# Attention in a four-branch decoder layer: values follow two score blocks behind, a third score bank, and the division and gate beside the third output pass

## The chip, the cores and the metric

One core of a Trainium2 chip runs the whole program. The metric is the device time of one execution in microseconds (us), as the median of several runs. Views of the profile come from one execution that was recorded.

## The reference, cut to what matters

One layer of a decoder takes 1024 prompt tokens and 8 sample tokens (width 2048) through one input projection, then through four groups of heads: A (gated delta rule), B (RWKV-7), C (forgetting attention) and D (pooling). Each group's output is multiplied by a gate, and one output projection with LayerNorm ends the layer. Group C and the end are what the change touches:

```python
s = jnp.einsum('nqhd,nshd->nhqs', qb, k) * (HEAD_DIM ** -0.5)
s = s + jnp.swapaxes(cqb, 1, 2)[..., :, None] - jnp.swapaxes(ck, 1, 2)[..., None, :]
s = jnp.where((kpos[None, :] <= qpos[:, None])[None, None], s, NEG_INF)
return jnp.einsum('nhqs,nshd->nqhd', jax.nn.softmax(s, axis=-1), v)
...
gated = jnp.concatenate([o_A * _silu(z_A), o_B * _silu(z_B), o_C * _silu(z_C), o_D * _silu(z_D)], axis=-1)
out = jnp.einsum('nte,ed->ntd', gated, P['w_out'])
y = _layernorm(ALPHA_DN * x + out, P['ln_g'], P['ln_b'])
```

Group C has 8 heads of 64 numbers; c is the running sum of the log forget gates. The 8 sample tokens attend to 4096 cached positions each.

## The kernel before, in words

All is float32; a product of two float32 matrices is made as three matmuls of parts (high and low: whi, wlo, xh, xl; ph, pl for the weights of the softmax). Nobody writes the order of an engine's instructions by hand: a scheduler fixes it when the program is built, from dependences, priorities and its own estimate of times. Side work ("fillers", generators given to `add` with a rate) is put between the instructions of the main work by `fill`, a few steps each time. Each engine then carries out its list in order and waits at an instruction whose inputs are late.

Stage by stage: input projection with the branches A, B and D as side work (to about 1717 us), then the attention stage `mixing` (1717 to 1920 us), then four output passes in the order D, B, A, C: three `out_pass` and `out_last`, which also does the LayerNorm.

In the attention stage `branch_c` goes through the 8 heads. In `c_attend` a head has two blocks of 512 queries; for each block of 128 keys TensorE makes the scores transposed (L849 with the low parts, L850 with the high parts and four rows of offsets, L853 or L855 the causal mask) into a PSUM bank "s", ScalarE takes the exponential into cpt (L859, three buffers) and rounds it to cph (L860), VectorE makes the remainder cpl (L861), and three matmuls L868 to L870 add weights times values into a bank "v". These value matmuls are held back by `late_values`: they come after the scores of the next LEAD blocks.

While head h runs, `c_scores(h + 2)` is a filler that prepares head h+2: loads on ScalarE's queue, ckk by GpSimd (L825, L826), and `c_max`, which finds each query's largest score. That is 12 blocks of matmuls (L785, mask L788) into banks "b" and "m", each read by a reduction on VectorE into cmx (L789); then cm (L792), a transpose on TensorE (L794), cmt on ScalarE (L796), its parts cmh and cml on VectorE (L798, L799), DMAs on ScalarE's queue (L831) into cmr, and a cast on VectorE into the offset rows of cqx (L832), in two halves of 512 queries. The scores L850 of head h+2 read cqx. A second filler, `decode_v`, streams cached values (dkv) through TensorE for the sample tokens (L1105).

The banks of `mixing` are "s", "v" and "m" with CBANKS of each, "b" with two and "k" with one. `c_max` and the value transposes ask `ctag` for a bank, which cycles over "b", "b" and "m".

When two heads are done, `c_gate` divides and gates their outputs at once: cden = exp(-log den) on ScalarE (L908), cnum times cden (L911) and times the gate cz (L912) on GpSimd over 128x1024, and a DMA into the DRAM array G (L913). An output pass reads its group's part of G with `gated` (L1694 to L1696: a load, gh on ScalarE, gl on VectorE). In the third pass VectorE adds ALPHA times x (L1714) and the sums from PSUM (L1720) to y; the weights' parts are cast by ScalarE and VectorE (L302, L303).

Of the kernel before, what the change touches and what calls it, by code (L numbers as in the profile page):

```python
# [6 lines left out]
F32 = mybir.dt.float32  # L7
# [3 lines left out]
AF = mybir.ActivationFunctionType  # L11
# [4 lines left out]
T = 1024  # L16
# [8 lines left out]
NPOOL = {392: 8, 384: 10, 256: 8}  # L25
VBUFS = 5, 4
RATE_L = 1.6
LEAD = 1
CBANKS = 2, 2, 1
RATE_C = 1.1  # L30
AHEAD = 2000
RATE_V = 0.7, 1.5
# [147 lines left out]
class Kernel:  # L180
# [14 lines left out]

    def ps(self, tag="a", shape=(128, 512)):
        pool, bufs = {"pj": (self.psum1, 3), "a": (self.psum1, 2), "o": (self.psum1, 5), "s": (self.psum1, CBANKS[0]),
                      "v": (self.psum1, CBANKS[1]), "m": (self.psum1, CBANKS[2]), "b": (self.psum0, 2), "k": (self.psum0, 1)}[tag]
        return self.t(pool, list(shape), tag, F32, bufs=bufs)

    def c(self, name, rows=slice(0, 128)):
# [702 lines left out]
        self.late_values()  # L904

    def c_gate(self, pool, hp, num, den):
        nc = self.nc
        nc.scalar.activation(den, den, AF.Exp, scale=-1.0)  # L908
        z = self.t(pool, [128, T], "cz", bufs=1)
        nc.gpsimd.dma_start(z, self.O["pj"][CZ + hp, :, :T])  # L910
        nc.gpsimd.tensor_tensor(num, num, den, op=ALU.mult)  # L911
        nc.gpsimd.tensor_tensor(num, num, z, op=ALU.mult)  # L912
        nc.gpsimd.dma_start(self.G[8 + hp, :, :T], num)  # L913


    def pages(self, pool, bufs, lead):
# [867 lines left out]
    def build(self):  # L1784
# [8 lines left out]
        self.gr = tc.dram_tile([8, N], F32, name="grow")  # L1793
        self.br = tc.dram_tile([8, N], F32, name="brow")
        self.UT = tc.dram_tile([4, 16, 32, 32], F32, name="ut")
        self.lfd = tc.dram_tile([8, 32, 1024], F32, name="lfd")
        self.crow = tc.dram_tile([8, 4, T], F32, name="crow")
        self.sco = tc.dram_tile([128, 4097], F32, name="sco")
# [7 lines left out]
        with P(name="const", bufs=1) as cp, P(name="psum", bufs=2, space=PSUM) as self.psum0:  # L1806
            with P(name="psum1", bufs=2, space=PSUM) as self.psum1:
                with P(name="w", bufs=2) as wp, P(name="x", bufs=1) as xp:
                    a, b = w(self.seq[0]), w(self.seq[1])
                    self.weights(wp, [c for p in zip(a, b) for c in p] + [c for t in self.seq[2:] for c in w(t)], 2)  # L1810
                    self.weight(0)
                    with P(name="stage", bufs=4) as sp:
                        self.load_x(xp, sp)
                        self.setup(cp, sp)
                        self.inputs(cp, sp)
                    with P(name="stage2", bufs=2) as sp:
                        self.inputs_cd(sp)
            dv = P(name="dv", bufs=1)
            vp = dv.__enter__()
            with P(name="psumc", bufs=2, space=PSUM) as self.psum1, P(name="c2", bufs=1) as c2, P(name="c1", bufs=1) as c1, \  # L1820
                    P(name="c", bufs=2) as cpool:
                self.cp += [c1, c2]
                self.mixing(vp, cpool)
            self.c0.__exit__(None, None, None)
            with P(name="psum2", bufs=2, space=PSUM) as self.psum1:
                R = dict(side="right")
                with P(name="wo", bufs=2, **R) as wp, P(name="ost", bufs=2, **R) as sp, P(name="y", bufs=1, **R) as yp, \
                        P(name="g2", bufs=1, **R) as g2:
                    self.y = [self.t(yp, [128, N], f"y{c}") for c in range(16)]
                    order = (3, 1, 0, 2)  # L1830
                    self.weights(wp, [self.I["wo"][ct][:, 4 * br:4 * br + 4] for br in order for ct in range(16)], 1, 48)
                    with P(name="g1", bufs=1) as g1:
                        g = [self.gated(3, g1, sp)]
                        with P(name="posta", bufs=1) as pp:
                            post = self.post_chain_a(pp)
                            self.add(post, RATE_P)
                            self.out_pass(0, g[0], sp)
                            self.drain(post)
                        g.append(self.gated(1, g2, sp))
                        with P(name="smpA", bufs=1) as pp:  # L1840
                            smp = self.sample_a(pp)
                            self.add(smp, RATE_P)
                            self.out_pass(1, g[1], sp)
                            self.drain(smp)
                        g.append(self.gated(0, g1, sp))
                        self.out_pass(2, g[2], sp)
                        self.drain()
                        g.append(self.gated(2, g2, sp))
                    dv.__exit__(None, None, None)
                    with P(name="wres", bufs=1) as rp:  # L1850
                        self.keep = rp
                        self.out_last(3, g[3], sp, rp)
# [63 lines left out]

    def mixing(self, vp, cpool):

        tags = itertools.cycle(("b",) * 2 + ("m",) * CBANKS[2])
        self.ctag = lambda: next(tags)  # L1920
        self.add(self.decode_v(vp), RATE_V[0])
        self.branch_c(cpool)
        for f in self.fillers:
# [43 lines left out]
```

## Time and profile before

| what | value |
|---|---|
| median of 3 runs | 2395.63 us (2390.84 to 2396.36) |
| profiled execution | 2396.94 us, of which its span on the core is 2395.2 us |
| TensorE busy over the span | 95% |
| VectorE, ScalarE, GpSimd busy | 57%, 39%, 12% |
| mean granted TensorE clock | 0.979 |

The span is the stretch from the first to the last recorded instruction; 1.74 us of the execution lie around it. A busy share averages over stages. The granted clock is 1.0 at 2.4 GHz and 0.5 at 1.2 GHz; a mean between them says how much of a stretch was spent at the lower one. An entry like "[2.31 <-DVE cmx L789]" in a row says that the engine stood idle for 2.31 us before this instruction, until VectorE's instruction of line 789 had made cmx.

### The profile page before, as it was taken

The numbers are of one execution on the slowest core, as the hardware profiler recorded it, in microseconds if no ns is written. First come the engines' busy times: TensorE is split into PE (matmuls) and PEld (weight loads), VectorE is DVE, ScalarE is ACT, GpSimd is POOL, SyncE is SP. The second block draws the span as 40 slices with busy tenths as digits, with TensorE's granted clock in tenths as the row PEclk, the third lists the DMA queues.
The fourth block names the chain that finished last, engine by engine and source line by source line (L and its number), as shares of the span: only waits on it lengthen the run. The fifth ranks groups of instructions, "written<-read, shape, count | busy, mean of one in ns | idle before, by whom it ended". The sixth has DMA issues, their size and how long they took to land. (4 is left out here: it accounts for less than half of the span.)

```text
span 2395.2 us, 47251 instructions
## 1 busy us (share of the span) xinstructions
PE 2282.6 (95%) x17640; PEld 2023.0 (84%) x17640; DVE 1364.7 (57%) x2676; ACT 938.4 (39%) x1853; POOL 295.0 (12%) x408
## 2 busy tenths in 40 slices
PE   8999999999899999999999999999899999999984
PEld 8999999998899999787787877899755578889984
DVE  4665757677576557432222245555578644564598
ACT  5644445434454444121111122454366665211244
POOL 0000000000000000103111121100132110100175
PEclk9999999999999999999999999999999999999997
DMA  6133323545523336778878888653488775683212
GB/s 215 56 100 95 104 85 95 151 106 120 113 81 94 89 107 142 172 187 264 274 250 283 259 273 288 232 161 107 124 260 248 223 282 192 219 304 129 88 63 88
DMA packets 369664, 402.44 MB, mean 168 GB/s; under 512 B 204877, under 2 KB 228350, under 8 KB 368666
## 3 DMA queue, kind: packets, MB, share of 16 engines
q1 hardware_dynamic: 307698, 263.83, 37.3%
q10 hardware_dynamic: 50056, 101.60, 13.9%
q0 software_dynamic: 11680, 33.99, 4.3%
q8 instruction: 139, 2.28, 0.4%
q14 instruction: 91, 0.75, 0.1%
HBM read 314.56 MB, written 84.67 MB: 167 GB/s over the span
## 5 line engine op out<-in xcount | busy, mean ns | idle before, releaser
L308 PE MATMUL pj<-xh,wlo 128*128 128x344 f32 x2688 | 873.1, 326 | 16.7 <-DVE wlo L303 8.6
L309 PE MATMUL pj<-xl,whi 128*128 128x344 f32 x2688 | 871.5, 324 | 0.0
L310 PE MATMUL pj<-xh,whi 128*128 128x344 f32 x2688 | 865.2, 324 | 0.0
L308 PEld LDWEIGHTS pj<-xh,wlo 128*128 128x128 f32 x2688 | 508.1, 189 | 37.1 <-issue 11.4
L309 PEld LDWEIGHTS pj<-xl,whi 128*128 128x128 f32 x2688 | 508.5, 189 | 19.8 <-issue 14.4
L310 PEld LDWEIGHTS pj<-xh,whi 128*128 128x128 f32 x2688 | 507.9, 189 | 16.4 <-issue 13.1
L302 ACT CAST whi<-raw 128x256 fp32r<-128x256 f32 (+1 forms) x504 | 213.0, 424 | 732.6 <-PE pj L310 530.2
L303 DVE TENSOR_TENSOR wlo<-raw,whi 128x256 fp32r<-128x256 f32 (+1 forms) x504 | 226.8, 452 | 365.5 <-ACT whi L302 356.1
L309 PE MATMUL o<-gl,whi 128*128 128x344 f32 x576 | 185.8, 323 | 0.0
L308 PE MATMUL o<-gh,wlo 128*128 128x344 f32 x576 | 184.6, 325 | 0.8 <-ACT gh L1695 0.5
L310 PE MATMUL o<-gh,whi 128*128 128x344 f32 x576 | 185.1, 321 | 0.0
L308 PEld LDWEIGHTS o<-gh,wlo 128*128 128x128 f32 x576 | 107.9, 188 | 21.8 <-DVE y L1720 9.4
L309 PEld LDWEIGHTS o<-gl,whi 128*128 128x128 f32 x576 | 109.0, 189 | 2.3 <-DVE ps L1221 0.9
L310 PEld LDWEIGHTS o<-gh,whi 128*128 128x128 f32 x576 | 109.0, 189 | 0.8 <-issue 0.8
L365 ACT ACTIVATE stg<-pj 128x344 f32<-128x344 f32 x168 | 74.6, 457 | 74.2 <-PE pj L310 73.0
L997 PE MATMUL k<-dkv,dqb 128*32 128x256 f32 x1024 | 88.4, 394 | 15.1 <-DMA dkv<-in_ck 9.0
L1720 DVE TENSOR_TENSOR y<-y,o 128x344 f32<-128x344 f32 x96 | 48.0, 510 | 57.3 <-PE o L310 57.0
L1105 PE MATMUL k<-dkv,dpT 128*8 128x512 f32 x512 | 71.5, 635 | 0.8 <-DMA dkv<-in_cv 0.8
L861 DVE TENSOR_TENSOR cpl<-cpt,cph 128x512 fp32r<-128x512 f32 (+1 forms) x96 | 60.9, 653 | 15.7 <-ACT cph L860 14.9
L308 PE MATMUL o<-gh,wkl 128*128 128x392 f32 (+2 forms) x192 | 63.9, 333 | 0.6 <-DVE wkl L303 0.5
L310 PE MATMUL o<-gh,wkh 128*128 128x392 f32 (+2 forms) x192 | 63.6, 331 | 0.0
L309 PE MATMUL o<-gl,wkh 128*128 128x392 f32 (+2 forms) x192 | 63.3, 330 | 0.0
(597 smaller groups left out, 3321.9 us busy)
## 6 DMA issues: line engine op xcount, KB each, us to landing
dkv<-in_ck SPq DMA_DIRECT2D x256, 256.0 KB
dkv<-in_cv SPq DMA_DIRECT2D x256, 256.0 KB
raw<-in_w ACTq DMA_DIRECT2D x228, 256.0 KB
out_pj<-stg ACTq DMA_DIRECT2D x33, 516.0 KB
bop<-bop SPq DMA_DIRECT2D x16, 1024.0 KB
raw<-in_wo ACTq DMA_DIRECT2D x64, 256.0 KB
aop<-aop SPq DMA_DIRECT2D x16, 768.0 KB
aop<-aost SPq DMA_DIRECT2D x40, 256.0 KB
```

The costliest lines, as they stand in the source:

```text
L302: nc.scalar.copy(hi, raw)
L303: nc.vector.tensor_tensor(lo, raw, hi.bitcast(F32), op=ALU.subtract)
L308: nc.tensor.matmul(ps, lhsT=wlo, rhs=xh, start=start, stop=False)
L309: nc.tensor.matmul(ps, lhsT=whi, rhs=xl, start=False, stop=False)
L310: self.last = nc.tensor.matmul(ps, lhsT=whi, rhs=xh, start=False, stop=stop).ins
L365: self.nc.scalar.activation(dst[:, g * G3:g * G3 + G3], ps[g], func)
L861: nc.vector.tensor_tensor(pl[:, off:], pt[:, off:], ph[:, off:].bitcast(F32), op=ALU.subtract)
L997: nc.tensor.matmul(ps[32 * hp:32 * hp + 32], lhsT=qb[:, hp, b], rhs=kt[:, :, hp], start=b == 0, stop=b == 7)
L1105: mm = lambda i: nc.tensor.matmul(po[32 * i:32 * i + 8], lhsT=pTv[:, c, :, 4 * bg + i], rhs=t[i // 2][:, i % 2], start=False, stop=c == 31)
L1720: nc.vector.tensor_tensor(y[:, s], y[:, s], ps[g], op=ALU.add)
```

## The change

`LEAD` goes from 1 to 2: the value matmuls of a block come after the scores of the next two. The score banks "s" go from two to three, and bank "m" is given up for it, so that `c_max`, its transpose and the value transposes use the two banks "b" alone. `c_gate` now only writes numerator and log denominator into two new DRAM arrays. The division and the gate become `gate_c`, a filler beside the third output pass, in eight pieces of 128x512: three loads on GpSimd's queue, an exponential, two products on GpSimd, a store into G.

```diff
-LEAD = 1
-CBANKS = 2, 2, 1
+LEAD = 2
+CBANKS = 3, 2
...
-                      "v": (self.psum1, CBANKS[1]), "m": (self.psum1, CBANKS[2]), "b": (self.psum0, 2), "k": (self.psum0, 1)}[tag]
+                      "v": (self.psum1, CBANKS[1]), "b": (self.psum0, 2), "k": (self.psum0, 1)}[tag]
...
     def c_gate(self, pool, hp, num, den):
-        nc = self.nc
-        nc.scalar.activation(den, den, AF.Exp, scale=-1.0)
-        z = self.t(pool, [128, T], "cz", bufs=1)
-        nc.gpsimd.dma_start(z, self.O["pj"][CZ + hp, :, :T])
-        nc.gpsimd.tensor_tensor(num, num, den, op=ALU.mult)
-        nc.gpsimd.tensor_tensor(num, num, z, op=ALU.mult)
-        nc.gpsimd.dma_start(self.G[8 + hp, :, :T], num)
+        self.nc.gpsimd.dma_start(self.CN[hp], num)
+        self.nc.gpsimd.dma_start(self.CD[hp], den)
+
+    def gate_c(self, pool):
+
+        nc = self.nc
+        for hp in range(4):
+            for s in (slice(0, 512), slice(512, 1024)):
+                o, d, z = (self.t(pool, [128, 512], x, bufs=2) for x in ("gn", "gd", "gz"))
+                nc.gpsimd.dma_start(o, self.CN[hp, :, s])
+                nc.gpsimd.dma_start(d, self.CD[hp, :, s])
+                nc.gpsimd.dma_start(z, self.O["pj"][CZ + hp, :, s])
+                nc.scalar.activation(d, d, AF.Exp, scale=-1.0)
+                nc.gpsimd.tensor_tensor(o, o, d, op=ALU.mult)
+                nc.gpsimd.tensor_tensor(o, o, z, op=ALU.mult)
+                nc.gpsimd.dma_start(self.G[8 + hp, :, s], o)
+                yield 1
...
-                        self.out_pass(2, g[2], sp)
-                        self.drain()
+                        with P(name="gatec", bufs=1) as pp:
+                            self.add(self.gate_c(pp), RATE_P)
+                            self.out_pass(2, g[2], sp)
+                            self.drain()
...
-        tags = itertools.cycle(("b",) * 2 + ("m",) * CBANKS[2])
-        self.ctag = lambda: next(tags)
+        self.ctag = lambda: "b"
```

The scheduler makes a new order from this. Three places of it follow. A row gives a line, an operation, what it writes and what it reads, with buffer numbers. Lines of the changed kernel are one lower than before up to the function `c_gate`, so that L784, L787, L793, L848, L849 and L867 to L869 are the L785, L788, L794, L849, L850 and L868 to L870 of before.

The first place is TensorE early in the stage, in head 0. Before, the values (v) of a block follow one block (s) behind:

```order
L849 MATMUL s_21505<-cqq_20424,ckk_20423 128x512
L850 MATMUL s_21505<-cqx_20425,ckx_20414 128x512
...
L870 MATMUL v_21349<-cpl_21345,cvh_20294 128x384
L868 MATMUL v_21349<-cph_21410,cvl_20295 128x256
L869 MATMUL v_21349<-cph_21410,cvh_20294 128x256
L870 MATMUL v_21349<-cpl_21411,cvh_20294 128x256
L868 MATMUL v_21349<-cph_21427,cvl_20295 128x256
L869 MATMUL v_21349<-cph_21427,cvh_20294 128x256
L849 MATMUL s_21522<-cqq_20424,ckk_20423 128x512
L850 MATMUL s_21522<-cqx_20425,ckx_20414 128x512
```

In the changed kernel the same stretch reads:

```order
L848 MATMUL s_21502<-cqq_20426,ckk_20425 128x512
L849 MATMUL s_21502<-cqx_20427,ckx_20416 128x512
L869 MATMUL v_21413<-cpl_21182,cvh_20296 128x512
...
L869 MATMUL v_21413<-cpl_21409,cvh_20296 128x256
L848 MATMUL s_21520<-cqq_20426,ckk_20425 128x512
L849 MATMUL s_21520<-cqx_20427,ckx_20416 128x512
L848 MATMUL s_21537<-cqq_20426,ckk_20425 128x512
L849 MATMUL s_21537<-cqx_20427,ckx_20416 128x512
L848 MATMUL s_21602<-cqq_20426,ckk_20425 128x512
L849 MATMUL s_21602<-cqx_20427,ckx_20416 128x512
```

Score blocks now stand in bunches of up to three, with the values of earlier blocks between the bunches.

The second place is TensorE at the transpose L794 of head 6, whose cqx is number 23160 (scores and values that follow are those of head 5). Before, the order goes on with score and value blocks:

```order
L794 MATMUL b_23513<-cst_211,cm_3271_23511 8x128
L785 MATMUL b_23652<-ckx_23557,cqm_23558 128x256
L788 LDWEIGHTS identb_19787
L788 MATMUL b_23652<-mq_19789,identb_19787 128x128
L870 MATMUL v_23583<-cpl_23579,cvh_22229 128x384
L868 MATMUL v_23583<-cph_23644,cvl_22230 128x256
L869 MATMUL v_23583<-cph_23644,cvh_22229 128x256
L785 MATMUL m_23733<-ckx_23557,cqm_23558 128x512
...
L849 MATMUL s_23969<-cqq_23159,ckk_23158 128x512
L850 MATMUL s_23969<-cqx_23160,ckx_23149 128x512
```

From the first of these rows to the last, which reads cqx of head 6 for the first time, there are 74. In the changed kernel (cqx number 23150) there are 17:

```order
L793 MATMUL b_23504<-cst_213,cm_3269_23502 8x128
L784 MATMUL b_23625<-ckx_23546,cqm_23547 128x256
L787 LDWEIGHTS identb_19789
L787 MATMUL b_23625<-mq_19791,identb_19789 128x128
L784 MATMUL b_23643<-ckx_23546,cqm_23547 128x256
...
L784 MATMUL b_23660<-ckx_23546,cqm_23547 128x384
...
L784 MATMUL b_23722<-ckx_23546,cqm_23547 128x512
...
L784 MATMUL b_23740<-ckx_23546,cqm_23547 128x512
L784 MATMUL b_23743<-ckx_23546,cqm_23547 128x256
...
L849 MATMUL s_23958<-cqx_23150,ckx_23139 128x512
```

The `c_max` blocks of head 7 (ckx number 23546) have moved into one bunch between the transpose and the scores of head 6.

The third place is GpSimd. Before, the two products of a head pair stand between the preparations of two heads:

```order
L777 MEMSET cmx_22709 128x16
L911 TENSOR_TENSOR cnum_21172<-cnum_21172,cden_21173 128x1024
L912 TENSOR_TENSOR cnum_21172<-cnum_21172,cz_22178 128x1024
L913 DMA gated<-cnum_21172 128x1024
L910 DMA cz_23102<-out_pj 128x1024
L825 TENSOR_TENSOR ckk_22688<-ckr_22677,ckx_22679 64x1024
```

In the changed kernel only the two writes stand there, and the products have gone behind the last DMA of the second pass (out_oAS):

```order
L906 DMA cn<-cnum_21174 128x1024
L907 DMA cd<-cden_21175 128x1024
L776 MEMSET cmx_22703 128x16
L824 TENSOR_TENSOR ckk_22681<-ckr_22670,ckx_22672 64x1024
...
L1492 DMA out_oAS<-sS_26418 128x2048
L915 DMA gn_27927<-cn 128x512
L916 DMA gd_27928<-cd 128x512
L917 DMA gz_27929<-out_pj 128x512
...
L919 TENSOR_TENSOR gn_27927<-gn_27927,gd_27928 128x512
L920 TENSOR_TENSOR gn_27927<-gn_27927,gz_27929 128x512
L921 DMA gated<-gn_27927 128x512
```

## Rows read from the trace of the kernel before

**Rows 1.** The page: span, and each engine's busy time, share and count.

```profile
span 2395.2 us, 47251 instructions
PE 2282.6 (95%) x17640; PEld 2023.0 (84%) x17640; DVE 1364.7 (57%) x2676; ACT 938.4 (39%) x1853; POOL 295.0 (12%) x408
```

**Rows 2.** Windows: attention stage, two pieces of it, passes two and three.

```profile
core 0: us, PE busy (x) PEld busy (x) DVE busy (x) ACT busy (x) POOL busy (x), PEclk, DMA share, GB/s
1717.00:1920.00 203.00, 181.58 (x1000) 106.14 (x998) 155.18 (x267) 132.00 (x258) 48.69 (x34) 0.92 0.83 249
1783.00:1807.00 24.00, 20.83 (x125) 12.75 (x126) 22.67 (x37) 16.35 (x35) 9.96 (x7) 1.00 0.89 272
1874.00:1898.00 24.00, 19.55 (x103) 11.71 (x103) 12.72 (x18) 13.64 (x29) 5.88 (x4) 0.86 0.71 217
2040.00:2246.00 206.00, 204.81 (x1345) 183.18 (x1343) 113.95 (x211) 36.01 (x61) 9.70 (x17) 1.00 0.58 195
```

**Rows 3.** Waits of PE's weight loads in 1717 to 1920: total us, times, longest.

```profile
PEld v L870 <- DVE cpl L861: 10.0, 8, 4.7
PEld s L849 <- ACT cpt L859: 8.9, 6, 2.9
PEld v L868 <- ACT cpt L859: 5.1, 6, 0.9
PEld v L868 <- ACT cph L860: 3.2, 5, 1.0
```

**Rows 4.** Timeline at a `c_gate`, all engines: start, duration, instruction, [idle before].

```profile
1834.37 2.35 POOL L911 TENSOR_TENSOR cnum<-cnum,cden 128x1024 f32<-128x1024 f32 x1 [3.27 <-ACT cden L908]
1834.96 1.91 DVE L799 TENSOR_TENSOR cml<-cmt,cmh 8x128 fp32r<-8x128 f32 x1
1836.80 0.41 DVE L789 TENSOR_REDUCE cmx<-m 128x1 f32<-128x256 f32 x1
...
1837.46 0.44 PE L785 MATMUL b<-ckx,cqm 66*128 66x384 f32 x1 [2.31 <-DVE cmx L789]
```

**Rows 5.** Timeline at the next `c_gate`, and two rows away from one.

```profile
1880.75 2.40 POOL L912 TENSOR_TENSOR cnum<-cnum,cz 128x1024 f32<-128x1024 f32 x1
1880.98 2.45 DVE L861 TENSOR_TENSOR cpl<-cpt,cph 128x256 fp32r<-128x256 f32 x1
...
1883.48 0.58 PE L870 MATMUL v<-cpl,cvh 128*128 128x256 f32 x1 [4.45 <-DVE cpl L861]
...
1731.32 0.41 DVE L861 TENSOR_TENSOR cpl<-cpt,cph 128x256 fp32r<-128x256 f32 x1
...
1860.27 0.27 DVE L799 TENSOR_TENSOR cml<-cmt,cmh 8x128 fp32r<-8x128 f32 x1
```

**Rows 6.** Windows of 10 us around those two places (columns as in rows 2).

```profile
1830.00:1840.00 10.00, 7.64 (x45) 3.92 (x43) 8.36 (x17) 7.67 (x17) 5.36 (x4) 0.89 0.80 239
1880.00:1890.00 10.00, 6.52 (x22) 3.33 (x22) 6.72 (x8) 3.94 (x7) 4.20 (x4) 0.66 0.68 216
```

**Rows 7.** Timeline: transposes and offset casts of head 6, then of head 2.

```profile
1857.59 0.27 PE L794 MATMUL b<-cst,cm 128*8 128x128 f32 x1
...
1863.09 0.42 DVE L832 CAST cqx<-cmr 4x512 fp32r<-4x512 f32 x1
...
1866.99 0.42 DVE L832 CAST cqx<-cmr 4x512 fp32r<-4x512 f32 x1
...
1762.40 0.27 PE L794 MATMUL m<-cst,cm 128*8 128x128 f32 x1
...
1770.25 0.42 DVE L832 CAST cqx<-cmr 4x512 fp32r<-4x512 f32 x1
...
1776.47 0.42 DVE L832 CAST cqx<-cmr 4x512 fp32r<-4x512 f32 x1
```

**Rows 8.** Timeline of GpSimd in 2125 to 2210, passes two and three.

```profile
2206.10 0.75 POOL L1121 DMA_DIRECT2D gated<-dzs  x1 [74.30 <-DVE dzs L1120]
```

**Rows 9.** Third pass: VectorE's y by lines, and the tile gl.

```profile
L1714 DVE SCALAR_TENSOR_TENSOR y<-ostg,y 128x1032 f32<-128x1032 f32 x16 | 19.7, 1231 | 16.6 <-DMA ostg<-in_xT 16.5
...
L309 PE MATMUL o<-gl,wkh x5: 338/342/342, 2246.7 to 2249.5; 128*128 128x392 f32 x5
L1696 DVE TENSOR_TENSOR gl<-ostg,gh x4: 1233/1234/1236, 2213.2 to 2221.6; 128x1032 fp32r<-128x1032 f32 x4
```

More of the change, by code (lines that the diff above doesn't have):

```diff
@@ L1 @@
-import itertools
 import math
@@ L1795, in build @@
         self.UT = tc.dram_tile([4, 16, 32, 32], F32, name="ut")
+        self.CN = tc.dram_tile([4, 128, T], F32, name="cn")
+        self.CD = tc.dram_tile([4, 128, T], F32, name="cd")
         self.lfd = tc.dram_tile([8, 32, 1024], F32, name="lfd")
```

## The prediction

> **What bounds the kernel now.** I read the page first: TensorE (PE) is busy for 95% of the span, VectorE (DVE) 57%, ScalarE (ACT) 39%, GpSimd (POOL) 12% [rows 1]. So a gain must come from a stretch in which PE stands still or is slowed. The windows show which. In the second and third pass PE is busy 204.81 of 206 us at granted clock 1.00 [rows 2]: there is nothing to gain there, only something to spoil. In the attention stage it is busy 181.58 of 203 us at clock 0.92 [rows 2]: about 21 us idle, and if the clock's mean of 0.92 lies between its two levels of 2.4 and 1.2 GHz, another 0.08 x 203 = 16 us of it were given up to the lower one. The change edits this stage, and moves its last step into the third pass.
>
> Inside the stage no single engine bounds. In 1783 to 1807 DVE is busy 22.67 of 24 us (94%), but in 1874 to 1898 only 12.72 (53%) with PE at 19.55 [rows 2]. So I read next the waits, which say what PE stands still for. Four of them are of the pipeline score, exponential, remainder, values: values for cpl 10.0 us, scores for the exponential that frees their bank 8.9, values for cpt and cph 5.1 and 3.2 [rows 3], together 27.2 us. Last I read the timeline where the longest ones stand.
>
> **What the change does, part by part.** (a) *GpSimd's two products leave the stage.* They are four pairs of 2.35 and 2.40 us [rows 4, 5]. At 1834.37 the first product runs, and VectorE's cml takes 1.91 us where it takes 0.27 elsewhere [rows 4, 5]; the reduction from PSUM at 1836.80 beside the next product takes 0.41, so it is not disturbed. At 1880.98 cpl takes 2.45 us where 0.41 is usual [rows 5]. What follows on PE: `c_max` stands 2.31 us for a bank whose reduction was queued behind that cml [rows 4], and the values stand 4.45 us for that cpl [rows 5]. After each, the granted clock of the 10 us is 0.89 and 0.66 [rows 6], which costs about 10 x 0.11 = 1.1 and 10 x 0.34 = 3.4 us. Sum 2.31 + 4.45 + 1.1 + 3.4 = 11.3 us. The stage also loses four exponentials of 128x1024 on ACT, which is busy 132 of 203 us [rows 2] and so gives back a little; I take −12 in all. Bounds: if other waits step in, only the excess durations come back, 1.6 + 2.0 = 3.6 us (−4); −13 if ACT's share is double.
>
> The Trainium skill (page "SBUF — State Buffer", sections "Who interferes with whom" and "SBUF: two separate sides") says that a VectorE instruction with two SBUF inputs, or a cast in a two-port mode, contends with a GpSimd instruction that reads SBUF, that the later one waits for the earlier one's whole length, and that a reduction never does on this chip. By that rule, the trace agrees: 1.91 and 2.45 us beside 0.41 for the reduction [rows 4, 5]. The rule speaks against the new place as well; it is the third rival.
>
> (b) *Values two blocks behind, and a third score bank.* Before, PE could run one block ahead of ACT and DVE; now it can run two. Of the 27.2 us of pipeline waits [rows 3], 4.45 are in (a) already, and the longest for cpt, 2.9, is the start-up of the stage, where nothing is ahead yet; 27.2 − 4.45 − 2.9 = 20 us remain. A deeper queue can remove a wait that comes from jitter, but not one where DVE is simply full, as in 1783 to 1807. I take three quarters, −15; bounds −5 (only the waits away from the full stretches) and −20.
>
> (c) *The scheduler's order gives up cover at the start of a head.* From the transpose L794 to the second cast into cqx a chain runs over ACT, DVE, a DMA, DVE, and again a DMA: head 6 needs 5.9 us to its first cast's end and 9.8 to its second; head 2 8.3 and 14.5 [rows 7] (1863.09 + 0.42 − 1857.59; the others likewise). I take head 6's, rounded to 6 and 10, since head 2's stands at the start of the stage's crowded middle. Before, 74 rows of PE's order stood between the transpose and the first score that reads cqx; now 17 stand there for head 6. What PE has to do in them: a matmul of 344 columns takes 204.81 / 1345 = 0.152 us in the passes [rows 2], so 512 columns about 0.23. The rows shown for head 6 are blocks of 256, 256, 384, 512, 512 and 256 columns and five masks of 128, 2816 columns or 1.3 us. The same count over the order of the changed kernel gives, for heads 2 to 7, 9.5, 8.0, 3.0, 5.7, 1.3 and 0.9 us up to the first score, and 15.9, 12.8, 6.3, 8.8, 5.6 and 4.1 up to the fifth block, which needs the second half. Against 6 us, heads 4 to 7 wait 3.0, 0.3, 4.7 and 5.1 = 13.1 us; against 10 us the second halves add about 0.7 for head 4, 0.9 for head 5 and little for heads 6 and 7, whose wait has already shifted them. Sum +15. With a chain shorter by a seventh it is +12; with head 2's lengths it is +35, the second rival. Three of these stalls are as long as the 4.45 us after which the clock fell; at 1.1 to 3.4 us for each [rows 6] that is 3 to 10 us, and I take +3, since the work behind them is dense.
>
> (d) *Two banks instead of three for `c_max`.* A block then needs the reduction of the block two before, 0.4 to 0.7 us of DVE. The order is alternated with other PE work nearly everywhere; where it is not, it is the bunch inside head 6's and head 7's chain, during which PE would wait for cqx anyway. Its cover is that wait, so 0; without it some 5 us.
>
> (e) *Division and gate in the third pass.* GpSimd there stands still for 74.30 us before its one DMA at 2206.10 [rows 8], so eight pieces with half the product's 2.4 us twice each, 8 x 2 x 1.2 = 19 us, have room. VectorE has 114 of 206 us of work there [rows 2]. PE needs group C's gl from 2246.7; it was ready by 2221.6 + 1.2 = 2222.8 [rows 9], so 24 us of slack hide the gate as long as the last piece is not later than that. The risk is that VectorE's two-input instruction y = ALPHA x + y (L1714), 16 x 1.231 us [rows 9], is held up by GpSimd's products; PE does not wait for y unless its five banks are all full. Bounds 0 and +6, taken +1. In the stage itself one load and one store of a head pair give way to two stores of the same size, so nothing there.
>
> **The sum.** −12 − 15 + 15 + 3 + 0 + 1 = −8 us. The profiled execution took 2396.94 us, its span of 2395.2 and 1.74 around it; it lies 1.3 us above the median of the runs, 2395.63. The same −8 from that median gives 2388 us. What a measurement of this kernel tells from no change is about 0.3%, 7.2 us; so this is just beyond it.
>
> **The rivals.** First, *the freed middle*. Where DVE is 94% busy [rows 2], c_max blocks move later, into the stretch where it is half idle, and cml, cqx and cpl lose what GpSimd added; then (b) reaches its bound of −20 and (c) its lower 12 with a clock that stays up: −12 − 20 + 12 = −20, 2375 us. For it: the uneven load of DVE. Against it: c_max of heads 6 and 7 is moved exactly into the chains.
>
> Second, and on the other side, *the chain of the offsets becomes the stage's bound*. Place: PE at the first score of heads 4 to 7. If a chain takes as long as head 2's, 8.3 and 14.5 us [rows 7], PE waits 35 us and loses 6 by the clock, against −12 and −15 and part of (b) that has nothing to hide: 35 + 6 − 12 − 14 = +15, 2411 us. It decides from a chain of about 8 us to the first cast. For it: the chain's last links are DMAs on ACT's queue and DVE casts that queue behind others' work, and head 2's was that long. Against it: every chain but that was near 6, and the products that lengthen casts are gone.
>
> Third, *the gate spoils the third pass*. GpSimd's 19 us hold VectorE's y-additions and weight casts; if each piece costs PE a stall of 1 to 1.75 us, 8 to 14 us in all, the sum becomes 0 to +6: 2396 to 2402 us. By the rule of the Trainium skill named under (a), up to 19 us of VectorE's time would be blocked there. Against it: 24 us of slack, and 16 VectorE instructions of 1.231 us in some 100 us are the only large ones with two SBUF inputs.
>
> Fourth, *nothing is gained*: the pipeline waits only move from cpl and cpt to cqx, since ACT and DVE have the same work as before. (b) at −5 and (a) at −8 against +15 and +1 give about +3; with (b) between, −4 to +3: 2392 to 2399 us.
>
> **How the numbers follow.** Forecast 0.44 (its own range 2378 to 2396), freed middle 0.14, chain as the bound 0.15, spoiled third pass 0.05, nothing gained 0.22. Faster by more than 0.3% is below 2388.4: 0.34 of the forecast's 0.44 and the 0.14, 0.48. The rest of the forecast, 0.10, and the 0.22 are within it: 0.32. Slower is above 2402.8: 0.15 and 0.05, 0.20. The range goes from 2372, a little beyond the freed middle, to 2403; the chain as the bound is left out, and some 0.02 at either end.
>
> **What would show it.** Right: beside the stage no cml, cqx or cpl above 1 us; the waits of values for cpl and of scores for cpt at a quarter of [rows 3]; PE's longest waits at the first scores of heads 4, 6 and 7, for VectorE's cqx, of 3 to 5 us each; attention stage 9 us shorter, third pass unchanged within 2 us, and gl of group C ready before its first matmul. Wrong: waits for cqx of 7 us or more, or none; waits of L784 for cmx away from these places; holes on PE in the third pass.

## The result

The changed kernel takes 2409.0 us (median of 12 runs, 2400.77 to 2416.5) where the kernel before takes 2395.99 (12 runs, 2385.15 to 2407.89): a ratio of 1.0056, 95% interval 1.0034 to 1.0077. It is slower, by 13 us. The forecast was 2388, within 2372 to 2403.

The page of the changed kernel, its span and the engines' busy time (to [rows 1]):

```profile
span 2404.5 us, 47346 instructions
PE 2291.2 (95%) x17640; PEld 2025.9 (84%) x17640; DVE 1362.4 (57%) x2676; ACT 939.6 (39%) x1857; POOL 314.3 (13%) x448
```

TensorE has as many matmuls and was busy 8.6 us longer. To see where, I cut the trace at three events: the last matmul of the projection, the last values matmul of attention, and the first matmuls of the first and of the fourth output pass. Before, that gives these windows (columns as in rows 2), the attention stretch and passes one to three:

```profile
1717.20:1919.50 202.30, 180.99 (x997) 105.81 (x996) 155.10 (x266) 131.31 (x257) 48.69 (x34) 0.92 0.83 249
1920.40:2246.50 326.10, 320.83 (x2063) 284.88 (x2064) 170.17 (x287) 104.90 (x190) 26.60 (x41) 0.99 0.61 208
```

In the changed kernel the same, with the 4 us between them, and two pieces of the attention stretch:

```profile
1716.40:1925.90 209.50, 187.00 (x979) 111.00 (x977) 148.93 (x265) 127.15 (x253) 33.47 (x28) 0.89 0.77 232
1925.90:1929.90 4.00, 3.19 (x22) 0.65 (x22) 1.58 (x4) 1.47 (x3) 1.08 (x2) 1.00 1.02 407
1929.90:2256.70 326.80, 320.11 (x2063) 283.21 (x2064) 174.30 (x286) 108.73 (x197) 60.33 (x86) 1.00 0.69 235
...
1826.00:1836.00 10.00, 8.36 (x27) 4.32 (x26) 5.30 (x11) 3.37 (x8) 0.00 (x0) 0.50 0.31 108
1876.00:1886.00 10.00, 9.78 (x36) 3.94 (x35) 6.21 (x13) 3.54 (x8) 0.00 (x0) 0.50 0.43 138
```

The passes did not move: 326.1 us and 326.8. The attention stretch and the few us behind it went from 203.2 to 213.5 us, and that is all of the loss in this execution. Idle time (length less PE's busy time) is 21.3 us before and 22.5 after. What grew is the time given up to the lower clock, length times (1 − granted clock): 202.3 x 0.08 = 16 us before, 209.5 x 0.11 = 23 us after. The two parts overlap where PE stands idle at the lower clock, so their sum is an upper bound. The two pieces show how it looks: PE is busy nearly throughout and runs at 1.2 GHz. In 1876 to 1886 it carries out 36 matmuls at that clock.

The waits of PE's weight loads in 1717 to 1930 of the changed kernel (to [rows 3]):

```profile
PEld v L869 <- DVE cpl L860: 8.5, 10, 2.1
PEld s L849 <- DVE cqx L831: 7.5, 4, 3.4
PEld b L784 <- DVE cmx L788: 5.8, 10, 1.5
PEld b L784 <- DVE cpl L860: 5.1, 5, 1.7
PEld v L867 <- ACT cph L859: 4.9, 5, 1.7
PEld s L848 <- ACT cpt L858: 3.9, 2, 2.2
...
PEld b L784 <- DVE cqx L831: 1.7, 1, 1.7
...
PEld v L867 <- ACT cpt L858: 0.9, 1, 0.9
```

Two kinds of wait have grown: scores for cqx, and `c_max` (L784) for a bank behind cmx and cpl. Scores waiting for cqx are new. Its longest case is head 7 in the timeline of the changed kernel: the transpose L793, the two casts of the offsets, and the first scores that read them:

```profile
1900.34 0.27 PE L793 MATMUL b<-cst,cm 128*8 128x128 f32 x1
...
1904.15 0.42 DVE L831 CAST cqx<-cmr 4x512 fp32r<-4x512 f32 x1 [2.00 <-DMA cmr<-cml]
...
1904.63 0.56 PE L849 MATMUL s<-cqx,ckx 68*128 68x512 f32 x1 [3.19 <-DVE cqx L831]
...
1907.01 0.42 DVE L831 CAST cqx<-cmr 4x512 fp32r<-4x512 f32 x1 [2.43 <-DMA cmr<-cml]
1907.07 0.69 PE L849 MATMUL s<-cqx,ckx 68*128 68x384 f32 x1
```

The matmul of 384 columns takes 0.69 us there; [rows 4] has one of 384 columns at 0.44. The granted clock is 0.98 in 1903 to 1905 and 0.50 in 1905 to 1907: it fell behind the wait.

In the third pass the gate did what was forecast of it. The tile gl and VectorE's y = ALPHA x + y, to [rows 9]:

```profile
L308 PE MATMUL o<-gl,wkh x14: 335/340/345, 2256.9 to 2264.7; 128*128 128x392 f32 x14
L1705 DVE TENSOR_TENSOR gl<-ostg,gh x4: 1228/1233/1234, 2226.8 to 2234.6; 128x1032 fp32r<-128x1032 f32 x4
...
L1723 DVE SCALAR_TENSOR_TENSOR y<-ostg,y 128x1032 f32<-128x1032 f32 x16 | 24.5, 1533 | 12.6 <-DMA ostg<-in_xT 12.4
```

VectorE's two-input instruction takes 1533 ns in the mean where it took 1231, 4.8 us over 16 of them. The mean hides two cases: four of the 16 run beside a product of GpSimd and take 2.32 to 2.58 us, the other twelve take 1.22 to 1.24. One of the four with its product:

```profile
2157.91 1.30 POOL L920 TENSOR_TENSOR gn<-gn,gz 128x512 f32<-128x512 f32 x1
2157.92 2.38 DVE L1723 SCALAR_TENSOR_TENSOR y<-ostg,y 128x1032 f32<-128x1032 f32 x1 [3.11 <-DMA ostg<-in_xT]
```

In the passes neither matmuls nor weight loads wait for this instruction, and gl is ready 21 us before it is read.

### The profile page after: what moved, and what is told of

The parts are those of the page before. It is cut to its first block, busy times and chain, and to the rows that moved or that the text cites. A ratio compares the mean times of both kernels' runs of the same rounds, so it can differ in the third digit from the quotient of the medians.

```text
span 2404.5 us, 47346 instructions
## 1 busy us (share of the span) xinstructions
PE 2291.2 (95%) x17640; PEld 2025.9 (84%) x17640; DVE 1362.4 (57%) x2676; ACT 939.6 (39%) x1857; POOL 314.3 (13%) x448
## 4 chain that ended last, share of the span: by engine, by line
PE 76%; DMA 11%; DVE 7%; SPq 2%; ACT 2%; issue 2%; ACTq 0%; DVEq 0%; POOL 0%; POOLq 0%
PE pj L307 16%; PE pj L308 16%; PE pj L309 15%; PE o L307 3%; PE o L308 3%; PE o L309 3%; PE k L1006 3%; DMA dkv<-in_ck 3%; PE k L1114 2%; DMA raw<-in_wo 1%; DVE y L1760 1%; DVE y L1759 1%; PE a L612 1%; PE s L849 1%; DMA ostg<-gated 1%
## 5 line engine op out<-in xcount | busy, mean ns | idle before, releaser
L307 PEld LDWEIGHTS pj<-xh,wlo 128*128 128x128 f32 x2688 | 507.0, 189 | 35.6 <-issue 11.4
L308 PEld LDWEIGHTS pj<-xl,whi 128*128 128x128 f32 x2688 | 507.9, 189 | 20.6 <-issue 15.1
L309 PEld LDWEIGHTS pj<-xh,whi 128*128 128x128 f32 x2688 | 507.2, 189 | 16.6 <-issue 13.3
L860 DVE TENSOR_TENSOR cpl<-cpt,cph 128x512 fp32r<-128x512 f32 (+1 forms) x96 | 61.9, 663 | 20.6 <-ACT cph L859 19.8
L858 ACT ACTIVATE cpt<-s 128x512 f32<-128x512 f32 (+1 forms) x96 | 47.3, 507 | 44.3 <-DVE cpl L860 10.8
```

The source lines that it names most:

```text
L307: nc.tensor.matmul(ps, lhsT=wlo, rhs=xh, start=start, stop=False)
L308: nc.tensor.matmul(ps, lhsT=whi, rhs=xl, start=False, stop=False)
L309: self.last = nc.tensor.matmul(ps, lhsT=whi, rhs=xh, start=False, stop=stop).ins
L858: nc.scalar.activation(pt[:, off:], ps[:, off:], AF.Exp, scale=0.125)
L860: nc.vector.tensor_tensor(pl[:, off:], pt[:, off:], ph[:, off:].bitcast(F32), op=ALU.subtract)
```

## The experiments

All were timed in 5 rounds beside the kernel before. "Cover" is TensorE's work between the transpose of a head and the first scores that read its cqx, counted over the order with the durations of the trace; "short" is what is missing to a chain of 5.9 us, summed over heads 2 to 7. "Idle" and "clock" are the two parts of the attention stretch as above. Time and ratio come from all runs of a kernel; stretch, idle, clock and waits come from its one profiled execution.

| kernel | banks s, v, b+m | short us | time us | ratio (95%) | stretch us | idle, clock us | cqx waits us |
|---|---|---|---|---|---|---|---|
| before | 2, 2, 3 | 0 | 2396 | | 202.3 | 21.3, 16 | 0 |
| changed | 3, 2, 2 | 13 to 15 | 2409.0 | 1.0056 (1.0034 to 1.0077) | 209.5 | 22.5, 23 | 7.5 |
| e_gate | 2, 2, 3 | 0 | 2394.1 | 0.9972 (0.9959 to 0.9986) | 184.6 | 13.2, 6 | 0 |
| e_banks | 3, 2, 2 | 15 to 19 | 2430.6 | 1.0119 (1.0085 to 1.0152) | 235.2 | 31.6, 45 | 8.4 |
| e_22 | 2, 2, 2 | 5 to 6 | 2396.7 | 0.9995 (0.9977 to 1.0013) | 195.0 | 18.2, 10 | 0.7 |
| e_411 | 4, 1, 2 | 26 to 32 | 2441.2 | 1.0163 (1.0137 to 1.0190) | 244.4 | 33.2, 51 | 13.0 |
| e_311 | 3, 1, 3 | 3 to 4 | 2398.2 | 1.0006 (0.9991 to 1.0022) | 201.7 | 14.6, 24 | 0.2 |
| e_late | 2, 2, 3 | 14 | 2430.6 | 1.0149 (1.0119 to 1.0178) | 225.9 | 31.6, 25 | 9.0 |
| e_cover8 | 2, 2, 3 | 8.5 | 2401.9 | 1.0013 (0.9990 to 1.0036) | 194.9 | 20.6, 10 | 6.9 |
| e_cover17 | 2, 2, 3 | 17 | 2420.2 | 1.0092 (1.0060 to 1.0123) | 211.9 | 27.1, 25 | 12.7 |
| e_lead1 | 3, 2, 2 | 13 to 15 | 2408.3 | 1.0047 (1.0028 to 1.0065) | 212.4 | 19.3, 32 | 7.4 |
| e_rate | 2, 2, 3 | 0 | 2431.1 | 1.0144 (1.0118 to 1.0170) | 190.7 | 21.6, 15 | 0 |
| e_tail | 2, 2, 3 | 0 | 2387.0 | 0.9962 (0.9944 to 0.9980) | 184.0 | 13.3, 6 | 0 |

The waits for cqx are those of the scores within the stretch. The stretch's start varies between the profiled executions (1705.7 to 1721.1), so stretches say more than absolute times of one trace. The medians of before in the rounds of the experiments were 2399.68, 2396.51 and 2397.3 us, so kernels of different rounds are compared by their ratios. The profiled execution of e_cover17 is the fastest of its six (2401.6 us; median 2420.2), and its stage began 10 us before that of e_cover8.

The clock early in the stage differs between executions of one order: in the first 24 us it is 0.86 in the changed kernel and 0.58 in e_lead1. Behind these 24 us, e_gate, the changed kernel and e_cover17 show:

```profile
1745.10:1905.70 160.60, 153.31 (x913) 94.15 (x913) 123.61 (x232) 109.87 (x221) 25.47 (x23) 1.00 0.85 256
1740.40:1925.90 185.50, 169.63 (x890) 100.85 (x889) 127.88 (x232) 108.70 (x222) 24.30 (x24) 0.89 0.74 224
1729.70:1917.60 187.90, 165.90 (x885) 102.42 (x884) 124.66 (x229) 111.72 (x220) 22.72 (x23) 0.89 0.71 217
```

There e_gate loses nothing to the clock and is idle for 7.3 us; the changed kernel loses 20 us and is idle for 15.9, e_cover17 21 and 22.0.

**The gate move alone.** The changed kernel with `LEAD` and the banks as they were before:

```diff
-LEAD = 2
-CBANKS = 3, 2
+LEAD = 1
+CBANKS = 2, 2, 1
...
-        self.ctag = lambda: "b"
+        tags = itertools.cycle(("b",) * 2 + ("m",) * CBANKS[2])
+        self.ctag = lambda: next(tags)
```

> The kernel before with the gate move alone: two score banks, bank m kept, LEAD 1, c_gate writes two arrays and gate_c runs beside the third pass. The order of TensorE leaves 10.8 us or more of work between every transpose and the first scores that need it, so no wait for cqx. Theory chain (the changed kernel lost its time because the scheduler's order, with a third score bank and without bank m, puts the transposes late, so TensorE waits for cqx and for cmx; the gate move itself gains): 2384 to 2391, the attention stage (last projection matmul to first output matmul, 203.2 us before and 213.4 us in the changed kernel) at 191 to 198 us, the passes two and three as long as before within 1.5 us. Rival gate (the move of the gate costs, by its traffic and by GpSimd beside VectorE): 2400 or more. Rival banks-only-count (two instead of three banks for c_max): like theory chain here.

It is faster than before by 0.28%, 5.5 us against the median of before in the same rounds (2399.68), 3 us short of the range expected; its stage, 199.8 us to the first output matmul, lies above the 191 to 198 expected. Its windows, attention, the stretch behind it, and the passes:

```profile
1721.10:1905.70 184.60, 171.44 (x998) 103.86 (x997) 144.78 (x265) 128.04 (x252) 34.43 (x28) 0.97 0.86 261
1905.70:1920.90 15.20, 5.24 (x21) 0.85 (x19) 2.08 (x3) 3.51 (x5) 1.62 (x3) 0.64 0.96 364
1920.90:2246.20 325.30, 318.36 (x2045) 285.54 (x2046) 174.63 (x285) 106.67 (x194) 59.53 (x85) 0.99 0.67 225
```

Attention itself is 17.7 us shorter, half of it idle time and half the clock (0.97). But 14 of them are given back at once: between the last values matmul and the first output matmul there are 15.2 us where before had 0.9, on a DMA share of 0.96. The timeline of that stretch:

```profile
1905.71 0.28 PE L870 MATMUL v<-cpl,cvh 128*128 128x256 f32 x1
...
1910.37 1.05 SPq L1704 DMA_DIRECT2D ostg<-gated  x2
...
1919.80 1.05 ACT L1705 CAST gh<-ostg 128x1032 fp32r<-128x1032 f32 x1 [8.31 <-DMA ostg<-gated]
...
1920.91 1.80 PE L308 MATMUL o<-gh,wlo 128*128 128x344 f32 x5
```

SyncE issues the first two loads of the first pass's input behind six loads of cached pages, at 1910.37, and gh, which reads them, starts 9 us later. Among the waits of PE's weight loads in 1717 to 1930 are these:

```profile
PEld v L870 <- DVE cpl L861: 9.6, 13, 2.2
PEld v L868 <- ACT cph L860: 6.1, 6, 1.7
PEld v L868 <- ACT cpt L859: 5.1, 6, 0.9
PEld s L849 <- ACT cpt L859: 4.3, 4, 2.6
...
PEld b L785 <- DVE cmx L789: 0.6, 1, 0.6
```

**The bank edit alone**, with the gate left in the stage:

```diff
-        self.nc.gpsimd.dma_start(self.CN[hp], num)
-        self.nc.gpsimd.dma_start(self.CD[hp], den)
+        nc = self.nc
+        nc.scalar.activation(den, den, AF.Exp, scale=-1.0)
+        z = self.t(pool, [128, T], "cz", bufs=1)
+        nc.gpsimd.dma_start(z, self.O["pj"][CZ + hp, :, :T])
+        nc.gpsimd.tensor_tensor(num, num, den, op=ALU.mult)
+        nc.gpsimd.tensor_tensor(num, num, z, op=ALU.mult)
+        nc.gpsimd.dma_start(self.G[8 + hp, :, :T], num)
...
-                            self.add(self.gate_c(pp), RATE_P)
```

> The changed kernel with c_gate left whole in the stage, as before: LEAD 2, three score banks, no bank m. With LEAD at 1 the order of these banks is the same row for row, so this is the bank edit alone. Cover from transpose to first scores is 6.9, 7.8, 1.6, 3.1, 1.6 and 2.1 us for heads 2 to 7. Theory chain: slower than the changed kernel, 2412 to 2424, stage 216 to 226 us, since the bank edit costs 15 to 25 and the gate's gain is missing. Rival gate: 2392 to 2400, as before.

It is 1.19% slower than before, beyond the range expected, and so is its stage (241.0 us to the first output matmul). So the four corners of the change are known: the bank edit lengthens the attention stretch by 235.2 − 202.3 = 33 us with the gate in the stage, and by 209.5 − 184.6 = 25 us without; the gate move shortens it by 18 us and by 26. The passes stay at 325.7 us. The loss is the bank edit's, and the rival that blames the gate is out.

```profile
1716.50:1951.70 235.20, 203.59 (x977) 119.28 (x975) 157.60 (x264) 130.62 (x255) 46.72 (x34) 0.81 0.70 209
```

**LEAD.** The changed kernel with the old number:

```diff
-LEAD = 2
+LEAD = 1
```

> The changed kernel with LEAD back at 1. Its instructions stand in the same order on all five engines, row for row. Theory: the scheduler sorts value blocks by readiness, the number has no effect, and the time is that of the changed kernel, 2404 to 2413. Rival (the number delays values): 2395 to 2403, since attention would follow its scores more closely.

2408.3 us against 2409.0: `LEAD` does nothing with these banks. The order is the same row for row, and with the old banks and the gate moved LEAD 1 and 2 give one order too. (With the gate still in the stage, as in the kernel before, some rows do change place; no run times that.) The order of the changed kernel was made by the banks, and of the words of the change "values follow two blocks behind" is not a cause. The run is also a measure of noise: its stretch is 2.9 us longer than that of the changed kernel with other shares of idle and clock, since the clock stayed low in its first 24 us (0.58), where the changed kernel had 0.86.

**Two score banks, two for c_max.**

```diff
-CBANKS = 3, 2
+CBANKS = 2, 2
```

> The changed kernel with two score banks: bank m is gone and no third score bank is there, one PSUM bank stays unused. Cover to first scores 8.1, 9.2, 2.8, 10.7, 6.6 and 3.7 us, so against a chain of 5.9 us about 5 to 6 us are short in all, where the changed kernel is 13 to 15 us short. Theory chain: 2392 to 2400, stage 199 to 205 us, waits of scores for cqx under half of the 7.5 us of the changed kernel. Rival banks-only-count (it is the number of banks for c_max that costs, whatever the scores have): as slow as the changed kernel, 2405 to 2412. Rival gate: 2400 or more.

The time is as theory chain had it: no change against before. So the rival that makes the number of banks alone as costly as the whole change is out. But the stretch of 195.0 us is 10 us longer than that of e_gate, and the trace does not put this down to the chain: scores wait 0.7 us for cqx, while `c_max` waits 13.5 us for a bank behind cmx and cpl.

```profile
1720.60:1915.60 195.00, 176.81 (x999) 108.14 (x997) 146.21 (x264) 128.28 (x252) 33.44 (x28) 0.95 0.82 249
...
PEld b L784 <- DVE cmx L788: 8.4, 9, 2.6
PEld b L784 <- DVE cpl L860: 5.1, 5, 1.7
...
PEld s L849 <- DVE cqx L831: 0.7, 1, 0.7
```

So fewer banks for `c_max` have a price of their own. In the times it does not stand clear of noise: the ratio is 0.9995 (to 0.9977 at the least) and that of e_gate 0.9972 (to 0.9986 at the most). The third score bank, which takes nothing from `c_max`, adds a further 14.5 us of stretch; with it the waits for cqx go from 0.7 to 7.5 us and those of `c_max` for its banks from 13.5 to 10.9.

**Four score banks.**

```diff
-CBANKS = 3, 2
+CBANKS = 4, 1
```

> The changed kernel with four score banks, one bank for values and two for c_max. Cover to first scores 2.6, 1.9, 1.3, 1.2, 1.3 and 0.6 us: 26 to 32 us short. Theory chain: 2418 to 2435, stage 222 to 238 us, waits of scores for cqx two to three times the changed kernel's 7.5 us. Rival banks-only-count: like the changed kernel, 2405 to 2412. A single value bank may cost some us in either theory, where a block of queries ends; it would show as waits of the first values for cnum or cden.

Slower still, 2441 us, above the range, as is its stage; the waits for cqx, 13.0 us, are 1.7 times those of the changed kernel and not two to three times. More room for scores goes with a larger loss. The kernel also has one value bank for two; its sign, waits of the first values for cden, comes to 1.1 us.

```profile
1718.10:1962.50 244.40, 211.18 (x997) 122.47 (x997) 150.68 (x266) 129.61 (x255) 34.95 (x28) 0.79 0.69 207
```

**The chain late, all banks as before.** The decisive pair keeps two score banks and three for `c_max`, and only holds back the last steps of `c_max`, to block 5 (`kt` 4) or 4 (`kt` 3) of the second query half of the head ahead:

```diff
+        n, self.held = self.held, self.held + 1
+        while self.free <= n:
+            yield 1
         m8 = self.t(one, [128, 8], "cm8", bufs=2)
...
+            if qb and kt == 4 and self.prev:
+                self.free += 1
+                with self.tc.issue_after(mm.ins):
+                    for _ in self.prev:
+                        pass
+                self.prev = None
...
-                self.drain(g)
+                self.prev = g
```

> The kernel with the gate move alone, with all banks as before (two for scores, two for values, three for c_max), in which only the last steps of c_max (maximum of two, transpose, parts, DMAs, casts) are held back until the fifth block of the second query half of the head ahead of theirs. Cover from transpose to first scores 2.9, 3.7, 2.0, 3.8, 3.0 and 5.7 us for heads 2 to 7, 14 us short of a chain of 5.9 us in all, as the changed kernel is; in the gate move alone it is 10.8 us or more. Theory cover (the late transposes alone make the loss, by waits for cqx and the lower clock behind them): the stretch from the last projection matmul to the last value matmul grows from 184.6 us to 200 to 212, waits for cqx 6 to 12 us, granted clock 0.88 to 0.92, and the time is 2400 to 2410, since up to 10 us of the growth fall into the wait that the gate move has at the stage's end. Rival banks (fewer banks for c_max make the loss, the chain being hidden by other work): as the gate move alone, 185 to 190 us, 2390 to 2397.

> As e_late, banks as before and the gate moved, but the last steps of c_max are held back until the fourth block of the second query half, and they are put in without advancing the page filler, which in e_late put more page matmuls into the stage. Cover 3.4, 6.4, 4.4, 7.3, 1.4 and 6.7 us, 8.5 us short of a chain of 5.9 us in all. Theory cover: attention stretch 190 to 200 us where the gate move alone has 184.6, waits for cqx 2 to 6 us, 2394 to 2402. Rival banks: as the gate move alone, 183 to 188 us, 2390 to 2396.

> The same, held back one block further. Cover 2.3, 1.1, 1.8, 4.9, 2.6 and 5.6 us, 17 us short, a little more than the changed kernel's 13 to 15. Theory cover: attention stretch 205 to 218 us, waits for cqx 7 to 13 us, granted clock 0.85 to 0.91, 2402 to 2416. Rival banks: as the gate move alone, 183 to 188 us, 2390 to 2396. If e_late's 225.8 us came from its page matmuls waiting for transfers, this kernel is near 185 us too.

All three are slower than the gate move alone, though no bank was taken. e_late, the first, used `drain` in place of the inner loop, which put more page matmuls into the stage (1039 matmuls against 998); it is 20 us above its range, its 225.9 us hold 7.2 us of weight loads waiting for cached pages, and I set it aside. The two clean ones stand in the order of what is short:

```profile
1716.10:1911.00 194.90, 174.30 (x978) 105.83 (x976) 147.19 (x264) 129.41 (x251) 32.62 (x28) 0.95 0.80 246
```

for e_cover8, and for e_cover17

```profile
1705.70:1917.60 211.90, 184.77 (x978) 113.72 (x977) 145.71 (x264) 130.06 (x251) 31.69 (x28) 0.88 0.73 225
```

e_cover17 has the stretch of the changed kernel (209.5 us and, in e_lead1, 212.4) and its loss by the clock, with the banks of before; its idle time is larger, 27.1 us against 22.5 and 19.3. Its waits for cqx (first row) lead its list and are larger than the changed kernel's 7.5:

```profile
PEld s L853 <- DVE cqx L835: 12.7, 7, 6.5
PEld v L871 <- ACT cph L863: 8.8, 4, 4.3
```

The rival "number of banks for c_max" asked for 183 to 188 us. So a late chain alone is enough for a loss of this size. It is not shown that the chain makes all of it in the changed kernel: there the waits of `c_max` for its two banks, 10.9 us, stand beside those for cqx, and the two were not separated further. e_cover8 lies at the upper edge of its range, with waits for cqx of 6.9 us where 2 to 6 were expected, and e_cover17 4 us above its own; stalls cost more than theory cover had allowed for.

**A third score bank that takes nothing from c_max.**

```diff
-CBANKS = 3, 2
+CBANKS = 3, 1, 1
```

with bank m kept, so that one value bank pays for it.

> The changed kernel with three score banks, one value bank, and three banks for c_max (b, b, m). Cover 10.1, 10.3, 2.5, 13.6, 8.4 and 7.4 us: only head 4 is short, by 3.4 us. Theory cover: attention stretch 188 to 197 us, 2392 to 2399. If a third score bank is worth something by itself, as the prediction held, 175 to 184 us and 2385 to 2392. Rival banks: like the gate move alone, 185 us, unless the one value bank shows as waits of first values for cnum.

2398 us, no change against before and within the range of theory cover; its ratio to before is 1.0006 where that of the gate move alone is 0.9972, and its stretch is above the range. A gain from the third bank does not show. I don't read more from it: its waits for cqx are 0.2 us and its idle time is only 14.6, and some 10 of its 24 us of lost clock lie in its first 25 us. Why the clock takes the other 14 without waits for cqx is open, and so is the cost of a single value bank.

**The end of the stage.** Two kernels on top of the gate move:

```diff
-RATE_V = 0.7, 1.5
+RATE_V = 0.5, 1.5
```

> The gate move alone, with the cached values' pages at rate 0.5 for 0.7 in the attention stage, so that fewer of their matmuls and of their loads lie in the stage and more in the passes. Theory tail (in the gate move alone the stage's end is held by loads on a DMA share of 0.94, in which the first pass's input waits behind the pages): the 15.2 us between the last value matmul and the first output matmul shrink to under 8, the passes grow by what moved, at most 8 us, and the time is 2384 to 2392. Rival (the end is held by something else than the pages): the tail stays 13 to 20 us and the time is 2392 to 2400.

The stretch behind attention shrank from 15.2 to 3.9 us, as theory tail had it, but the passes went from 325.3 to 367.8 us and the time to 2431: a miss. The pages that left the stage came too late for the last pass, whose first sums waited 20.9 us in one piece:

```profile
PE o L1775 <- ACT ostg L1743: 20.9, 1, 20.9
```

The other moves the loads instead:

```diff
-            nc.sync.dma_start(r, self.G[4 * br + i])
+            (nc.scalar if br == 3 else nc.sync).dma_start(r, self.G[4 * br + i])
```

> The gate move alone, with the four loads of the first pass's input (ostg from group D's gate rows) on ScalarE's queue instead of SyncE's, where they stand behind six page loads. The order of TensorE in attention is the same. Theory queue: the loads start before the last attention steps, the tail shrinks from 15.2 to 4 to 8 us and the time falls to 2383 to 2390. Rival (the transfers themselves are late, since the DMA share is 0.94): tail 11 to 16 us, 2391 to 2397.

2387.0 us: 0.38% below before, in the range expected. The gate move alone was 0.28% below; the two intervals overlap, so that the times alone do not show a further gain. The trace shows what moved. On ScalarE's queue the two loads start at 1893.71 and 1894.09, before the last steps of attention, and the stretch behind it is 4.2 us:

```profile
1715.00:1899.00 184.00, 170.70 (x998) 104.11 (x997) 145.94 (x265) 128.04 (x252) 33.97 (x28) 0.97 0.85 263
1899.00:1903.20 4.20, 0.27 (x3) 0.07 (x1) 1.56 (x3) 1.67 (x3) 1.08 (x2) 0.98 1.03 401
1903.20:2235.00 331.80, 324.33 (x2064) 287.46 (x2065) 172.65 (x286) 109.04 (x197) 60.37 (x86) 0.98 0.68 232
```

Of the 11 us that the end gave back, 6.5 were lost again in the passes, which are 331.8 us long; in their first 37 us the clock is 0.82.

## Why the prediction was wrong

The reading of before held: the passes stayed full, and all of the difference lies in the attention stage. Step by step:

(a) *Gate out of the stage*, −12, bounds −4 to −13. Under-sized in attention, −17.7 us (e_gate), and over-sized for the program: 14 us of it ended in a wait for DMAs at the end of the stage that the prediction did not look for. "Where a stall goes, say what is late next" was not done: attention's end was taken for the stage's end. In the changed kernel the product pairs are gone, but some casts beside GpSimd's other work are still long, such as this one of cqx, 2.31 us where 0.42 is usual:

```profile
1767.68 2.38 POOL L824 TENSOR_TENSOR ckk<-ckr,ckx 64x1024 fp32r<-64x1024 f32 x1 [9.85 <-ACT ckx L768]
1768.03 2.31 DVE L831 CAST cqx<-cmr 4x512 fp32r<-4x512 f32 x1
```

(b) *Values two blocks behind and a third bank*, −15, bounds −5 and −20. **This is the step that failed first.** `LEAD` changes no row of the changed kernel's order. And the waits of the pipeline did not go: values for cpl, cph and cpt and scores for cpt were 27.2 us in [rows 3], 25.1 with the gate move alone (9.6, 6.1, 5.1 and 4.3) and 18.2 in the changed kernel (8.5, 4.9, 0.9 and 3.9): −7, near the bound of the smallest gain. e_311 and e_411 show no gain from more score banks either.

(c) *Cover given up*, +15 of waits and +3 of clock. The mechanism was right (e_cover17 shows that it alone can cost as much), the places in part: heads 4 and 7 waited, 1.7 and 3.4 us, head 6 did not, and heads 2 and 3, where no wait was expected, did for 1.2 us each. The waits came smaller: 7.5 us of scores and 1.7 of `c_max` for cqx. **The term for the clock was mis-sized**: +3, with a bound of 10, where the step from the gate move alone to the changed kernel took 23 − 6 = 17 us by the clock, beside 22.5 − 13.2 = 9 us of idle time. (Behind the first 24 us it is 20 us by the clock.) I had priced a stall's aftermath from two places in the kernel before, 1.1 and 3.4 us each. Here several waits follow one another in a bunch, and 10 us at half clock are 5 us lost; 1826 to 1836 and 1876 to 1886 alone make 10. Head 6 shows how: its bunch of `c_max`, priced at 1.3 us, takes about 4 at half clock, with a wait for a bank in it, which hides the chain of 4.1 us, and the loss moves from the wait to the work.

(d) *Two banks for c_max*, 0, bound 5. **Mis-sized too.** The waits of `c_max` for cmx and cpl are 10.9 us in the changed kernel (5.8 and 5.1) where the gate move alone has 0.6. Of the ten waits for cmx, six lie inside the chains of heads 4 and 6; the other four lie away from them, which the prediction had named as a sign of being wrong. e_22 is 10 us longer than e_gate in the stretch with hardly a wait for cqx. So it was not free, and the cover that I named for it was the same wait that (c) had already counted. Together (b), (c) and (d) stood in the sum at +3 us; the bank edit cost the stretch 25.

(e) *The gate in the third pass*, +1, bounds 0 and +6. Right: passes 326.8 us against 326.1, and four of the 16 two-input instructions slower by 1.1 to 1.4 us without a wait of PE for them. The Trainium skill (page "SBUF — State Buffer", section "Who interferes with whom") states that a VectorE instruction with two SBUF inputs contends with a GpSimd instruction that reads SBUF. The trace agrees: 2.32 to 2.58 us beside a product, 1.22 to 1.24 without, 4.8 us in all where the third rival had up to 19.

The second rival named the right side and nearly the time, 2411 us, but the time came out near by luck, from another split: 35 us of waits for cqx and 6 of clock, against 9 and 17. The chains of heads 2 to 4 were indeed long in the changed kernel, 9.9 to 11.4 us to the first cast, those of heads 6 and 7 only 4.1 and 4.2. Why the scheduler moves `c_max` behind the scores was not tried; the orders show only that it does so more with three and four score banks, where `c_max` has two, than with two (13 to 19 and 26 to 32 us short against 5 to 6).

## What to carry to other kernels

Where a scheduler makes the order, look at what a constant does to the order before pricing what it was meant to do: here one of two numbers did nothing, and giving a bank to one producer let it run ahead of the side chain that it needs itself. Price a new wait on TensorE with the lower clock behind it, and bunches of waits higher than single ones: e_late aside, the clock was more than half of the difference to the gate move wherever the stretch was longer by 15 us or more. And when a stage gets shorter, read what the next stage's first instruction waits for: most of the gain of the gate move was held by a load in a queue, and a line that moved the load took 11 us out of that end, of which the next passes lost 6.5 again.

## What the runs showed of the hardware

Over the kernels of the table, whose attention matmuls are the same but for some of the cached pages, the time lost to the lower clock ran from 6 to 51 us and the idle time from 13 to 33. In the changed kernel TensorE was busy for 1.26 of the 3 us from 1820, at a granted clock of 1.00, and stood idle for 1.34 us in them; from 1823 to 1836 the clock was 0.50, with TensorE busy 84% of the last 10 us. In 1876 to 1886, behind an idle time of 1.67 us, it was 0.50 too, with TensorE busy 98%. Two executions of one order differed as well: in the first 24 us of the stage the clock was 0.86 in the changed kernel and 0.58 in e_lead1. Four VectorE instructions of 128x1032 with two inputs took 2.32 to 2.58 us beside a GpSimd product of 1.30 to 1.71 us, and twelve without one 1.22 to 1.24.
